# A two-layer encoder trunk: the second layer's input product by one Strassen level on fp16 parts, its weights prepared and the up product's weight sums made by GpSimd

## The chip, the cores and the metric

The kernel runs on one core of one Trainium2 chip. The metric is the device time of one execution in microseconds; of three runs of the kernel before, the median is 2181.28 us (2181.2 to 2181.32). Engines are called by their names or short names: TensorE (PE, with its weight loads as PEld), VectorE (DVE), ScalarE (ACT), GpSimd (POOL) and SyncE (SP).

## The reference

1024 tokens of width 1024 pass two layers. Each layer has an attention with low-rank queries and keys beside a convolution module, then a gated feed-forward block with a short convolution. Cut to what is computed:

```python
D_MODEL, SEQ, DEPTH, D_FF = 1024, 1024, 2, 2816
for l in range(DEPTH):
    h = _rmsnorm(x, g_mix[l])
    p = h @ w_in[l]                       # 384 + 256 + 32 + 512 + 512 columns
    q = _rmsnorm(p[..., :o1], g_q[l]) @ w_uq[l]          # 8 heads, 64 + 32 rope
    kv = _rmsnorm(p[..., o1:o2], g_kv[l]) @ w_ukv[l]     # 8 heads, 64 + 64
    k_rope = _apply_rope(p[..., o2:o3], cos, sin)
    y_attn = _mla_attention(q_nope, q_rope, k_nope, k_rope, v)
    a, gt = jnp.split(p[..., o3:], 2, axis=-1)
    u = _dwconv(a * jax.nn.sigmoid(gt), w_dw_conv[l], b_dw_conv[l])   # 31 taps
    u = jax.nn.silu(_layernorm(u, g_conv_ln[l], b_conv_ln[l]))
    x = x + jnp.concatenate([y_attn, u], axis=-1) @ w_o[l]
    h2 = _rmsnorm(x, g_ffn[l])
    z = _dwconv(h2 @ w_up[l], w_dw_ffn[l], b_dw_ffn[l])  # 3 taps
    zg, zv = jnp.split(z, 2, axis=-1)
    x = x + (jax.nn.silu(zg) * zv) @ w_down[l]
return _rmsnorm(x, g_final)
```

The change concerns `h @ w_in[1]`, the second layer's input product, and the weights of the first layer's `h2 @ w_up[0]`.

## The kernel before, in words

**Form.** Everything is held transposed: channels on the 128 partitions, 1024 tokens in the free direction, in two halves of 512. The order of instructions on each engine is the order in which the program issues them. In the feed-forward block that order comes from an agenda: `put(step, rank, f)` files an action under one of TensorE's products (a step, about 2.6 us), and after each product its actions are issued by rank.

**Precision.** Each float32 operand is split into an upper and a lower part (hi, lo), and each product is three passes: hi by hi, hi by lo, lo by hi.

**Stages of a layer.** *Project*: the input product in 14 sections (gates g0 to g3, values a0 to a3 of the convolution, kv0 and kv1, the rope key kr, q0 to q2), then the keys k, queries' rope part u, queries n and values v, while the 31-tap convolution runs beside it. *Attention* of 8 heads, then the *output product* wo. *Up product*: 22 pairs of column groups, f = 0 to 21, each a gate half (e = 0) and a value half (e = 1) of 128 columns. *Down product*, whose results are added to x.

**The up product** is one Strassen level on fp16 parts: seven products of half size for each f, in the order (1, 2, 6, 5, 7, 3, 4) from f = 4 on, each 12 matmuls of 128x512 (L1306), 84 for an f. Products 1 and 2 use the weight block as it comes, the other five use sums of blocks. `raw[f][e]` (tiles `wu`) holds the fetched float32 block, and its sums are made in place, one after another, by DMAs that GpSimd issues and that add to the tile (`add_in`, L1196: `sum5`, `sum6`, `sum3`, `sum7`). After each, ScalarE scales and rounds the upper part (L1267), and VectorE makes the lower part (L1270), into tiles `w`. ScalarE takes the squares of each block (L1212); their total over partitions gives a power-of-two scale (`own_total`, `own_scale`). The results are evicted by ScalarE and VectorE (L1313, L1314), the three filter taps are VectorE's (L1766, tiles `o` and `v`), and L1186 holds `sub`, an addition of two tiles. The next block's sums begin while the former's products run.

**The second layer's input product** (`next_sections`, `inputs`, `shared_key`) is not Strassen. A section is 48 matmuls in float32 round form (L245, L558, L564), kr 32 (L810). The weights come by a casting DMA on GpSimd's queue (`cast`, L204); ScalarE writes the negative (L208) and a second, accumulating DMA makes the lower part (L209, `complete`). The moving operand is x times the gain g, split by L1732 and L1733 (`norm_apply`). The root of the mean square is found beside that (`norm_root`, L284 to L303), spread over the partitions (L322) and multiplied into the results as the row scale rx when they leave PSUM (L649, L652, L679, and in `key_rope`).

**The 31-tap convolution.** Near taps (NEAR_TAPS 12, 14, 15, 14 for the four channel groups, 55 in all) are VectorE's (`conv_step`, L2039). Far taps: ScalarE scales (L2045) and a DMA issued by GpSimd adds (L2046). Late taps, in the attention: GpSimd scales (L2056) and adds, either by itself (L2059) or by a DMA (L2061). Order and amounts come from tables and from a clock that the program counts up as it issues.

**The down product** (L1551) is Strassen too. Its last results are added to x by VectorE, x is stored, and the norm for the next layer is begun: squares, transposes and the root for the left half before the product ends, the right half after it.

Of the kernel before, what the change touches and what calls it, by code (L numbers as in the profile page):

```python
# [18 lines left out]
T = 1024  # L19
D = 1024  # L20
DEPTH = 2
# [102 lines left out]
WARM = 8  # L124

# [19 lines left out]
class Encoder:  # L145
# [32 lines left out]
    def weight_source(self, l, name):  # L178
        a = self.a
        kind, j = name[:-1], name[-1]  # L180
        if name == "kr":
            return a["w_kr"][l]
# [220 lines left out]
    def run(self):  # L403
# [11 lines left out]
        self.xd = [a["x"], self.dp.tile([8, 128, T], F32, name="x_mid")]  # L415
        carry = None
# [117 lines left out]
    def next_sections(self, l, nxt, supply):  # L534
        names = ("g0", "a0", "g1")
        w = [self.complete(*e) for e in nxt["w"]]
        for k in range(8):
            self.norm_apply(l, nxt["x"], nxt, 1, k)
        self.norm_sums(l, nxt["x"], nxt, 1, range(4, 8))
        supply(-16.0)  # L540
        self.pp.tile([128, T], F32, name=f"skip{l}", tag="w1", bufs=1)
        ps = [self.wide(f"p{n}{l}") for n in names]
        for c in range(2):
            for i in range(3):
                if (c, i) == (0, 0):
                    self.upper_first(ps[i], self.tiled(w[i]), nxt["hl"], HALVES[c])
                for k in range(8 if c or i else 0):
                    self.partial(ps[i], self.tiled(w[i]), nxt["hl"], k, (c,))
                if c == 1 and i == 0:
                    self.norm_root(l, nxt, 1, self.bank)  # L550
                if c == 1 and i == 1:
                    self.norm_spread(l, nxt, 1, self.bank)
        return nxt["hl"], nxt["r"], dict(zip(names, ps))

# [12 lines left out]
    def project(self, l, carry):  # L567
# [12 lines left out]
        outs = [(OUT_FROM + OUT_STEP * i, i, None) for i in range(4)]  # L580
        col = lambda i, n=1: qk[:, i:i + n]
# [19 lines left out]
        def key_scale():  # L601
            sums = self.bank(f"kt{l}", (128, 3))
# [40 lines left out]
        def start(steps):  # L643
            next(steps)
            active.append([clock["pe"] + 1.8, steps, 99])

# [8 lines left out]
        def glu(j):  # L655
# [7 lines left out]
            taps.extend((j, t) for t in todo[:NEAR_TAPS[j]])  # L663
            taps.sort(key=lambda e: NEAR_ORDER.index(e[0]))
            away[j] = todo[NEAR_TAPS[j]:]
# [11 lines left out]
        def latent(name, out, key, j):  # L677
            c = self.blk(f"c{name}{l}")
# [13 lines left out]
        def keys_norm():  # L692
            r = st["rkv"] = self.blk(f"rkv{l}")
            for s, p in zip(HALVES, self.spread(rooted("kroot"), f"rkv{l}", HALVES, self.bank)):
                nc.scalar.copy(out=r[:, s], in_=p)
# [1508 lines left out]
```

## Time and profile before

| | |
|---|---|
| median of three runs | 2181.28 us |
| span of the profiled execution | 2179.0 us |
| clock granted to TensorE in it | 1.00 in all but the last stage (0.99) |
| project, first layer | 0 to 200 us |
| attention, output product | 200 to 402, to 485 us |
| up product, first layer | 485 to 885 us |
| down product, first layer | 885 to 1087 us |
| project, second layer: input product | 1087 to 1239 us |
| keys, queries and values | 1239 to 1281 us |
| attention, output product | 1281 to 1470, to 1566 us |
| up product, second layer | 1566 to 1966 us |
| down product, last norm | 1966 to 2179 us |
| GpSimd's L1196 in the first up product | 80 DMA issues, 70.0 us |

The profiled execution's own time is its span; it lies 2.3 us below the median of the runs. Times in the text are from the span's start. A row of a group gives the line, engine and operation, the output and input tiles with numbers left out, their shapes and the count, then busy time and mean duration; a row of the timeline gives start and duration of single instructions, with the idle time before and what ended it in brackets.

### The profile page before, as it was taken

How to read it: one execution, taken by the hardware profiler on the slowest of the kernel's cores; microseconds unless marked ns; L12 is line 12 of the kernel's file. 1: busy time of each engine (PE TensorE's matmuls, PEld its weight loads, DVE VectorE, ACT ScalarE, POOL GpSimd, SP SyncE). 2: the span in 40 equal slices, each digit the busy share in tenths (PEclk: the TensorE clock that was granted, in tenths of full speed). 3: DMA queues.
4: the chain of work that ended last, by engine and by line, in shares of the span. 5: the costliest groups of instructions: out<-in, count | busy, mean ns of one | idle time of the engine just before them, and what ended most of it. 6: DMA issues, size and time to landing. Idle time of an engine off the chain costs nothing.

```text
span 2179.0 us, 29766 instructions
## 1 busy us (share of the span) xinstructions
PE 2169.7 (100%) x10722; PEld 1260.7 (58%) x10722; DVE 1844.7 (85%) x2531; ACT 1456.6 (67%) x2183; POOL 537.2 (25%) x534
## 2 busy tenths in 40 slices
PE   9999999999999999999999999999999999999998
PEld 8887665754444444644488876667544444446445
DVE  6989999879998887887859789998898888878877
ACT  6455888746898886554623668886478888865544
POOL 1223777211111111000012355771112111110000
PEclk9999999999999999999999999999999999999999
DMA  6898878754688885554578986886646888856533
GB/s 195 184 187 212 164 152 171 245 163 104 149 244 259 222 261 145 193 178 151 166 177 164 188 207 134 159 186 200 175 100 164 261 241 242 241 141 218 182 111 122
DMA packets 163013, 400.96 MB, mean 184 GB/s; under 512 B 21888, under 2 KB 29936, under 8 KB 162864
## 3 DMA queue, kind: packets, MB, share of 16 engines
q0 software_dynamic: 62528, 145.89, 36.4%
q1 hardware_dynamic: 100048, 252.63, 33.8%
q8 instruction: 84, 1.38, 0.3%
q10 hardware_dynamic: 288, 0.53, 0.1%
q14 instruction: 65, 0.53, 0.1%
HBM read 270.75 MB, written 69.66 MB: 156 GB/s over the span
## 4 chain that ended last, share of the span: by engine, by line
PE 98%; ACT 1%; DVE 1%; issue 0%; DMA 0%; DVEq 0%; ACTq 0%
PE p L1306 36%; PE pd L1551 18%; PE po L1026 7%; PE s L1818 7%; PE t L1858 5%; PE pq L245 3%; PE pa L245 3%; PE o L1880 2%; PE pkv L245 2%; PE pg L245 2%; PE pg L564 2%; PE pn L245 2%; PE o L1885 1%; PE pv L1794 1%; PE pk L245 1%; PE pa L564 1%
## 5 line engine op out<-in xcount | busy, mean ns | idle before, releaser
L1306 PE MATMUL p<-b,w 128*128 128x512 f16 x3696 | 800.0, 379 | 0.2
L1306 PEld LDWEIGHTS <-w 128*128 128x128 f16 x3696 | 358.7, 98 | 431.9 <-issue 0.8
L1551 PE MATMUL pd<-ab,wd 128*128 128x512 f16 (+2 forms) x1920 | 404.2, 373 | 0.0
L1196 POOL DMA_DIRECT2D wu<-in_w_up x176 | 152.2, 879 | 770.2 <-DVE w L1270 581.5
L1551 PEld LDWEIGHTS <-wd 128*128 128x128 f16 x1656 | 161.9, 98 | 179.4 <-issue 0.5
L1818 PE MATMUL s<-k,q 96*128 96x512 f16 x768 | 186.9, 379 | 0.0
L1270 DVE SCALAR_TENSOR_TENSOR w<-wu,wf,w 128x512 f16<-128x512 f32 (+1 forms) x216 | 177.2, 834 | 3.6 <-ACT w L1267 3.6
L1861 DVE SCALAR_TENSOR_TENSOR pt<-t,pt 128x512 f16<-128x512 f32 x256 | 163.0, 676 | 10.0 <-ACT pt L1860 9.0
L1267 ACT ACTIVATE w<-wu,wf 128x512 f16<-128x512 f32 (+1 forms) x216 | 164.8, 781 | 0.1
L1860 ACT ACTIVATE pt<-t 128x512 f16<-128x512 f32 x256 | 139.1, 596 | 32.0 <-PE t L1858 30.0
L1820 DVE TENSOR_REDUCE mx<-s 128x1 f32<-128x1024 f32 x128 | 155.0, 1211 | 1.0 <-PE s L1818 1.0
L1540 ACT ACTIVATE ab<-ac,ds 128x512 f16<-128x512 f32 x108 | 75.5, 717 | 108.7 <-DVE ac L1455 73.0
L1828 ACT ACTIVATE p<-s,mx 128x1024 f32<-128x1024 f32 x128 | 143.3, 1120 | 2.2 <-DVE mx L1820 1.8
L2039 DVE SCALAR_TENSOR_TENSOR conv<-gate,par,conv 128x1009 f32<-128x1009 f32 (+14 forms) x110 | 139.9, 1274 | 3.1 <-ACT conv L659 0.4
L2056 POOL TENSOR_SCALAR late<-gate,par 128x1019 f32<-128x1019 f32 (+13 forms) x99 | 135.5, 1368 | 27.2 <-PE pn L245 13.9
L1858 PE MATMUL t<-ident,p 128*128 128x128 f32 x1024 | 136.6, 275 | 0.9 <-ACT p L1828 0.6
L1858 PEld LDWEIGHTS t<-ident,p 128*128 128x128 f32 x1024 | 116.8, 141 | 34.8 <-issue 7.4
L1766 DVE SCALAR_TENSOR_TENSOR o<-zg,par,o 128x1023 f32<-128x1023 f32 x88 | 112.7, 1281 | 8.9 <-ACT o L1760 7.4
L1314 DVE SCALAR_TENSOR_TENSOR zg<-p,wf,zg 128x512 f32<-128x512 f32 x72 | 54.0, 750 | 71.2 <-PE p L1306 61.6
L1766 DVE SCALAR_TENSOR_TENSOR v<-zv,par,v 128x1023 f32<-128x1023 f32 x88 | 112.1, 1276 | 0.0
L1818 PEld LDWEIGHTS <-q 96*128 96x128 f16 x768 | 74.0, 97 | 64.6 <-issue 2.1
L1541 DVE SCALAR_TENSOR_TENSOR ab<-ac,ds,ab 128x512 f16<-128x512 f32 x108 | 79.9, 748 | 19.2 <-ACT ab L1540 19.2
(2179 smaller groups left out, 3814.1 us busy)
## 6 DMA issues: line engine op xcount, KB each, us to landing
wu<-in_w_up SPq DMA_DIRECT2D x98, 512.0 KB
wu<-in_w_up POOLq DMA_DIRECT2D x176, 256.0 KB, 4.8
sd<-in_w_down SPq DMA_DIRECT2D x44, 512.0 KB
ws<-sd SPq DMA_DIRECT2D x44, 512.0 KB
act<-v SPq DMA_DIRECT2D x36, 512.0 KB
ac<-act SPq DMA_DIRECT2D x72, 256.0 KB
wo<-in_w_o POOLq DMA_DIRECT2D x32, 256.0 KB, 7.7
x_mix<-y SPq DMA_DIRECT2D x32, 256.0 KB
```

Of the source, the lines that this page charges most:

```text
L245: nc.tensor.matmul(ps[:, HALVES[c]], w, x[:, HALVES[c]], start=(k == 0 and s == 0), stop=(k == n - 1 and s == 2))
L1026: self.nc.tensor.matmul(ps, p[:, sl], q[:, cs], start=(k == 0 and t == 0), stop=(k == 3 and t == 2))
L1196: nc.gpsimd.dma_start(out=dst, in_=src, accum_op=ALU.add)
L1267: nc.scalar.activation(out=t, in_=src, func=AF.Copy, scale=scale[f])
L1270: nc.vector.scalar_tensor_tensor(out=t, in0=src, scalar=scale[f], in1=hi, op0=ALU.mult, op1=ALU.subtract)
L1306: nc.tensor.matmul(ps, w[p][:, k * 128:(k + 1) * 128], b[:, q], start=(i in (1, 5, 2) and k == 0 and t == 0), stop=(k == 3 and t == 2), sk ...
L1551: nc.tensor.matmul(ps[t, m][:, cs], w[i, j][p][:, m * 128:(m + 1) * 128], b[:, q, cs], start=(i in (1, 5, 2) and j == 0 and s == 0), stop= ...
L1766: self.nc.vector.scalar_tensor_tensor(out=o[:, a:b], in0=z[:, at + a:at + b], scalar=self.par[l][:, tap:tap + 1], in1=o[:, a:b], op0=ALU.m ...
L1818: nc.tensor.matmul(ps[:, cs], q[0:96, i, qs], k[0:96, j, cs], start=(s == 0), stop=(s == 2))
L1820: nc.vector.tensor_reduce(out=mx, in_=ps, op=ALU.max, axis=AX.X, negate=True)
L1858: nc.tensor.transpose(tp[:, i, qi * 128:(qi + 1) * 128], st["p"][2 * qp + qi][:, kt * 128:(kt + 1) * 128], self.ident)
L1861: nc.vector.scalar_tensor_tensor(out=lo, in0=tp, scalar=P_SCALE, in1=hi, op0=ALU.mult, op1=ALU.subtract)
```

## The change

**The product.** For the second layer the 14 sections become seven column pairs (`PAIRED`): (g0, a0) to (g3, a3), (kv0, kv1), (q0, kr), (q1, q2); kr is padded to 128 columns. Each pair is one Strassen level of seven products, 49 in all in the order `PAIR_ORDER`, of 12 fp16 matmuls each. They run in `opening`, before the pool of PSUM tiles of the first layer's feed-forward is given back. `next_sections` goes.

**The moving operand.** x is multiplied by gain, a scale, and the root (`set_norm`) before it is split, so the results need no row scale. Its Strassen sums are made on VectorE (`set_mix`), the upper parts by ScalarE, the lower parts by VectorE (`set_end`).

**The weights.** They are prepared during the first layer's up product, a pair at each f of `PREPARE_AT`: SyncE fetches two blocks of 512 KB, ScalarE takes two squares, the scale comes with the up product's own (`own_total` has four columns there), GpSimd scales, combines, casts and subtracts (14 instructions for a pair), and SyncE stores the fp16 parts in DRAM (`win`, four stores), whence they are read back when needed.

**The up product's sums.** In the first layer, for f from 4 on, `sum5`, `sum6` and `sum3` are additions by GpSimd (`on_pool`) in place of accumulating DMAs; `sum7` stays a DMA.

**The convolution in the second layer.** 37 near taps (`PAIR_NEAR`) in place of 55; `side` gives GpSimd late taps during the projection, with its own sum, and far taps between; 52 late taps are left for the attention in place of 49. A step that a later product needs is brought forward by `settle`.

```diff
+PAIRED = (("g0", "a0"), ("g1", "a1"), ("g2", "a2"), ("g3", "a3"), ("kv0", "kv1"), ("q0", "kr"), ("q1", "q2"))
+PREPARED = ((1, 2), (5, 4), (6, 3), (7,))
+PREPARE_AT = (4, 7, 10, 13, 16, 18, 20)
+PAIR_NEAR = (11, 8, 10, 8)
...
+            def product(i, f):
...
+                for k in range(4):
+                    b = sets[i][k]
+                    for s, (x, y) in enumerate(((0, 0), (0, 1), (1, 0))):
+                        nc.tensor.matmul(p, t[:, x, k * 128:(k + 1) * 128], b[:, y], start=(i in (1, 5, 2) and k == 0 and s == 0),
+                                         stop=(k == 3 and s == 2), skip_group_check=i in (6, 7, 4, 3))
...
+            put(1, 3, lambda: self.norm_root(l, nxt, 1, lambda name: self.pp.tile([128, 512], F32, name=name, tag="d4", bufs=1)), 2.5)
+            put(2, 3, lambda: self.norm_spread(l, nxt, 1, lambda name: self.pp.tile([128, 512], F32, name=name, tag="d5", bufs=1)))
+            for i, ns in PAIR_MIX.items():
+                for e, n in enumerate(ns):
+                    put(n, 3, lambda i=i, e=e: mix(i, e), 1.2 * (i in (5, 3)) + 1.15 * (i != 3))
+                    put(n + 1, 2.5, lambda i=i, e=e: self.set_end(nxt, i, e), 1.28)
...
+                    if pool[0] <= clock["pe"]:
+                        next(self.tap_late(l, j, away[j].pop(0), u[j], conv[j], "both"), None)
+                        pool[0] = far_at[j] = clock["pe"] + 4.2
+                    elif more:
+                        self.tap_far(l, j, away[j].pop(0), u[j], conv[j])
...
+        def on_pool(f, h):
+            t = raw[f][1][:, left]
+            nc.gpsimd.tensor_tensor(out=t, in0=t, in1=raw[f][h[0]][:, HALVES[h[1]]], op=ALU.add)
+
         def sum5(f):
+            if ahead and f >= LEFT:
+                return on_pool(f, (1, 1))
             add_in(raw[f][1][:, left], block(f, 1, 1))
...
+            def scaled(e):
+                nc.gpsimd.tensor_scalar(out=two[e], in0=two[e], scalar1=z(33 + q), scalar2=1.0, op0=ALU.mult, op1=ALU.mult)
...
+            def hi(i):
+                src, k = both(i)
+                made[i] = self.blk(f"wit{q}{i}", F16, (128, k, 2, 512))
+                nc.gpsimd.tensor_copy(out=made[i][:, :, 0], in_=src)
+
+            def lo(i):
+                src, k = both(i)
+                nc.gpsimd.tensor_tensor(out=made[i][:, :, 1], in0=src, in1=made[i][:, :, 0], op=ALU.subtract)
+
+            def store(i):
+                nc.sync.dma_start(out=self.win[q][i], in_=made.pop(i))
...
+            work = ([lambda: scaled(0)], [lambda: scaled(1)], [lambda: hi(0)], [lambda: lo(0)],
+                    [lambda: plus(part(0, 0), part(1, 0)), lambda: hi(3)], [lambda: lo(3), lambda: plus(part(1, 0), part(1, 1))],
+                    [lambda: hi(1)], [lambda: lo(1), lambda: plus(part(0, 0), part(1, 1))],
+                    [lambda: plus(part(0, 1), part(0, 0)), lambda: hi(2)], [lambda: lo(2)])
...
+    def set_norm(self, nxt, c, k):
+        xk = nxt["x"][k][:, HALVES[c]]
+        self.nc.vector.scalar_tensor_tensor(out=xk, in0=xk, scalar=self.wz[:, k:k + 1], in1=nxt["r"][:, HALVES[c]],
+                                            op0=ALU.mult, op1=ALU.mult)
...
+    def set_end(self, nxt, i, e):
+        two, src = nxt["half"].pop((i, e))
+        self.nc.vector.tensor_tensor(out=two[:, :, 1], in0=src, in1=two[:, :, 0], op=ALU.subtract)
```

**How the order moves.** In the first layer's up product, about f = 12 to 15, GpSimd's queue before holds only DMA issues. `wu0_131` is the value half of f = 13 in the first layer; the last number is that of the allocation.

```order
L1196 DMA wu0_120_6219<-in_w_up 128x512
L1196 DMA wu0_131_6380<-in_w_up 128x512
L1196 DMA wu0_141_6539<-in_w_up 128x512
L1196 DMA wu0_131_6380<-in_w_up 128x512
L1196 DMA wu0_130_6378<-in_w_up 128x512
L1196 DMA wu0_141_6539<-in_w_up 128x512
L1196 DMA wu0_151_6694<-in_w_up 128x512
```

At the same place GpSimd's queue now reads so; `wi30` and `wi31` are the two blocks of the fourth column pair of the next layer, `wit30` and `wit33` their fp16 parts, `wz` the scales:

```order
L1378 TENSOR_TENSOR wu0_121_6341<-wu0_121_6341,wu0_120_6339 128x512
L1462 TENSOR_SCALAR wi30_6464<-wi30_6464,wz_103 128x1024
L1462 TENSOR_SCALAR wi31_6466<-wi31_6466,wz_103 128x1024
L1374 DMA wu0_120_6339<-in_w_up 128x512
L1378 TENSOR_TENSOR wu0_131_6516<-wu0_131_6516,wu0_130_6514 128x512
L1472 CAST wit30_6748<-wi30_6464 128x2x512
L1476 TENSOR_TENSOR wit30_6748<-wi30_6464,wit30_6748 128x2x512
L1378 TENSOR_TENSOR wu0_141_6683<-wu0_141_6683 128x512
L1449 TENSOR_TENSOR wi30_6464<-wi30_6464,wi31_6466 128x512
L1472 CAST wit33_6801<-wi30_6464 128x512
L1476 TENSOR_TENSOR wit33_6801<-wi30_6464,wit33_6801 128x512
L1449 TENSOR_TENSOR wi31_6466<-wi31_6466 128x512
```

Three of each block's four sums (L1378) have become instructions of GpSimd's own, and the preparation of the next layer's weights stands between them, ahead of sums that come later; the fourth sum is still a DMA (L1374).

In the second layer's projection, behind the input product, GpSimd's queue before holds weight fetches (`wk1`, `wu21`, `wq21`) and the adding DMAs of the far taps (`conv1_0` to `conv1_2` are the running sums of channel groups 0 to 2, and the number behind `far1_0` is the tap):

```order
L204 DMA wk1h_10535<-in_w_k 128x4x256
L209 DMA wq21l_10482<-in_w_in 128x1024
L2046 DMA conv1_0_10048<-far1_0_17_10590 128x1022
L2046 DMA conv1_1_10112<-far1_1_17_10593 128x1022
L2046 DMA conv1_2_10262<-far1_2_17_10596 128x1022
L204 DMA wu21h_10624<-in_w_uq 128x2x384
L209 DMA wk1l_10536<-in_w_k 128x4x256
```

There it now reads so, with the late taps' scalings (L2379, formerly L2056) and sums (L2382, formerly L2059) in between:

```order
L2379 TENSOR_SCALAR late1_0_14_10784<-zg0_10077,par1_183 128x1023
L2382 TENSOR_TENSOR conv1_0_10404<-conv1_0_10404,late1_0_14_10784 128x1023
L2379 TENSOR_SCALAR late1_2_11_10827<-zg2_10171,par1_183 128x1020
L2382 TENSOR_TENSOR conv1_2_10510<-conv1_2_10510,late1_2_11_10827 128x1020
L2369 DMA conv1_0_10404<-far1_0_16_10830 128x1023
L223 DMA wu21h_10860<-in_w_uq 128x2x384
L228 DMA wk1l_10757<-in_w_k 128x4x256
L2379 TENSOR_SCALAR late1_2_12_10881<-zg2_10171,par1_183 128x1021
L2382 TENSOR_TENSOR conv1_2_10510<-conv1_2_10510,late1_2_12_10881 128x1021
L2369 DMA conv1_0_10404<-far1_0_17_10918 128x1022
```

The weight fetches of the keys and queries (L223, L228, formerly L204, L209) now stand behind instructions of GpSimd's own.

398 lines of the change are left out of this document (322 added, 76 removed).

## The prediction

> **What bounds the kernel now.** I read the page's busy times first, then the chain that ended last, then the windows, then groups inside one stage.
>
> ```profile
> PE 2169.7 (100%) x10722; PEld 1260.7 (58%) x10722; DVE 1844.7 (85%) x2531; ACT 1456.6 (67%) x2183; POOL 537.2 (25%) x534
> PE 98%; ACT 1%; DVE 1%; issue 0%; DMA 0%; DVEq 0%; ACTq 0%
> L1306 PE MATMUL p<-b,w 128*128 128x512 f16 x3696 | 800.0, 379 | 0.2
> ```
>
> TensorE is busy for 2169.7 of 2179.0 us and carries 98% of the chain. The up products (L1306) wait 0.2 us in all. So every matmul taken out is worth its full time, and every new wait of TensorE costs its full time. Next, who keeps TensorE supplied, by stage (columns: length, then busy PE, PEld, DVE, ACT, POOL with counts, clock, DMA share, GB/s):
>
> ```profile
> 540.00:867.00 327.00, 326.88 (x1531) 148.31 (x1529) 280.93 (x395) 267.54 (x392) 62.04 (x71) 1.00 0.78 215
> 1087.00:1281.00 194.00, 193.71 (x877) 160.30 (x876) 151.20 (x162) 81.45 (x103) 45.99 (x52) 1.00 0.80 177
> 1281.00:1470.00 189.00, 188.57 (x1156) 114.82 (x1156) 171.90 (x226) 156.86 (x285) 135.98 (x112) 1.00 0.79 170
> ```
>
> The first row is the first layer's up product from the fifth column pair on: 18 pairs (f = 4 to 21). The second is the second layer's projections, the third its attention. In the up product VectorE has only 327.0 - 280.9 = 46.1 us free, and what it makes (lower weight parts, filter taps, evictions) is what TensorE waits for next.
>
> **The change part by part.** *TensorE.* One input section is 48 matmuls of 128x512, the rope section 32, one column pair of the up product 84:
>
> ```profile
> 1131.76 10.88 PE pg L245 x48
> 1197.04 7.25 PE pkr L810 x32
> 620.70 18.15 PE p L1306 x84
> ```
>
> Thirteen sections and the rope section go: 13 x 10.88 + 7.25 = 148.7 us for 656 matmuls at 0.227. In come 7 x 7 products of 12 matmuls, 588, of the up product's form at 18.15 / 84 = 0.216: 127.0 us. Gain 21.6 us. The transposes for the norm's root stay, four and four. With all else hidden the span would be 2179.0 - 21.6 = 2157.4. The profile's span lies 2.3 us under the median of the timed runs (2181.28), which I take as what lies around it: 2159.7.
>
> *The operand sets at the opening.* VectorE must scale the right half and make five combined sets in time:
>
> ```profile
> 1109.50 0.69 DVE L295 TENSOR_REDUCE rx_512v<-rx_512t 128x4 f32<-128x512 f32 x1 [13.18 <-PE rx_512t L284]
> 1111.42 0.16 DVE L300 SCALAR_TENSOR_TENSOR rx_512y<-rx_512q,rx_512y 128x4 f32<-128x4 f32 x1
> 1087.95 0.74 DVE L1733 SCALAR_TENSOR_TENSOR xs_0l<-x,par,xs_0h 128x512 fp32r<-128x512 f32 x1
> 1088.07 0.73 ACT L1732 ACTIVATE xs_7h<-x,par 128x512 fp32r<-128x512 f32 x1 [0.97 <-DVE x L1456]
> ```
>
> The root took 2.1 us (1109.50 to 1111.58). After the change its transposes follow two products (5.2 us), the scale is spread at about 9.3 us, and then come 8 norms (0.66 us start to start), 8 combinations and 10 lower parts of 1024 columns (1.14, group L1186 v below) and 8 evictions (0.66): 8 x 0.66 + 18 x 1.14 + 8 x 0.66 = 31 us, done near 40 us. The last set is needed at 16 products, 42 us. It fits, if narrowly; at the end of the first layer four lower parts (4.6 us) press against 3 us of free time. I take 1 us for both, between 0 and 4 (no gain is possible where TensorE does not wait now).
>
> *GpSimd in the up product.* This is the large term. It now makes 54 sums (three for each of 18 column pairs) in place of 54 DMA issues, and 98 instructions of weight preparation (14 for each of seven pairs). Its prices, from the attention and the last stage:
>
> ```profile
> 1321.35 2.34 POOL L2059 TENSOR_TENSOR conv<-conv,late 128x1016 f32<-128x1016 f32 x1
> 1323.67 1.10 POOL L2056 TENSOR_SCALAR late<-gate,par 128x1016 f32<-128x1016 f32 x1
> 2168.57 2.96 POOL L1738 TENSOR_TENSOR x<-x,rx 128x256 f32<-128x256 f32 x4 [222.70 <-ACT rx L1720]
> ```
>
> Two inputs cost 2.34 us for 1016 columns and 0.74 for 256; in between, 1.27 for 512. The sums are 54 x 1.27 = 69 us. A pair needs two scalings (1.10), casts of 3.5 x 1024 columns (no cast is in the trace; bounds 1.10 for one input and 2.34 for two; I take 1.10, as it has one input), subtractions of 3.5 x 1024 (3 x 2.34 + 1.27) and four sums (1.27): 2.2 + 3.9 + 8.3 + 5.1 = 19.5 us, for seven 136 us. Together 205 us of GpSimd in the 327 us where it issued DMAs alone. [...]
>
> GpSimd alone has room for 205 us. VectorE beside it has not. The one place in this trace where GpSimd computes next to VectorE instructions with both inputs in SBUF:
>
> ```profile
> 1269.83 1.22 DVE L798 SCALAR_TENSOR_TENSOR qns<-qn,qns 128x1024 f16<-128x1024 f32 x1
> 1274.65 3.06 DVE L798 SCALAR_TENSOR_TENSOR qns<-qn,qns 128x1024 f16<-128x1024 f32 x2
> 1277.63 1.21 DVE L794 TENSOR_TENSOR qn<-pn,rq 128x1024 f32<-128x1024 f32 x1
> 1280.01 2.23 DVE L798 SCALAR_TENSOR_TENSOR qns<-qn,qns 128x1024 f16<-128x1024 f32 x1 [1.17 <-ACT qns L796]
> ```
>
> ```profile
> 1274.36 1.14 POOL L2056 TENSOR_SCALAR late<-gate,par 128x1023 f32<-128x1023 f32 x1 [13.91 <-PE pn L245]
> 1276.41 2.25 POOL L2056 TENSOR_SCALAR late<-gate,par 128x1020 f32<-128x1020 f32 x1
> 1278.75 2.39 POOL L2059 TENSOR_TENSOR conv<-conv,late 128x1020 f32<-128x1020 f32 x1
> 1281.13 2.10 POOL L2056 TENSOR_SCALAR late<-gate,par 128x1019 f32<-128x1019 f32 x1
> ```
>
> L798 alone takes 1.22. At 1280.01 it met a running GpSimd sum and took 2.23: it ended 1.10 after that sum's end at 1281.14. GpSimd's next scaling took 2.10 instead of 1.10: it ended 0.99 after L798's end at 1282.24. They took turns. L794, one input of which is in PSUM, kept its 1.21 beside GpSimd. From 1274.36 to 1283.23, 8.87 us, stand three scalings, one sum and three L798, alone 3 x 1.10 + 2.34 + 3 x 1.22 = 9.30: the pair needs 0.95 of the two times added. In the up product VectorE does mostly the work that takes turns (12 column pairs, 620.70 to 838.56):
>
> ```profile
> L1270 DVE SCALAR_TENSOR_TENSOR w<-wu,wf,w 128x512 f16<-128x512 f32 x61 | 44.5, 746 | 0.6 <-ACT w L1267 0.6
> L1766 DVE SCALAR_TENSOR_TENSOR v<-zv,par,v 128x1023 f32<-128x1023 f32 x25 | 31.9, 1275 | 0.0
> L1766 DVE SCALAR_TENSOR_TENSOR o<-zg,par,o 128x1023 f32<-128x1023 f32 x24 | 30.8, 1282 | 1.3 <-ACT o L1760 0.7
> L1270 DVE SCALAR_TENSOR_TENSOR w<-wu,wf,w 128x1024 f16<-128x1024 f32 x12 | 15.3, 1276 | 0.0
> L1186 DVE TENSOR_TENSOR v<-v,o 128x1024 f32<-128x1024 f32 x12 | 14.6, 1217 | 0.0
> L1186 DVE TENSOR_TENSOR sd<-sd,sd 128x512 f32<-128x512 f32 x21 | 14.4, 685 | 0.0
> L1186 DVE TENSOR_TENSOR sd<-sd 128x512 f32<-128x512 f32 x21 | 14.4, 685 | 0.0
> 620.70:838.56 217.86, 217.86 (x1021) 98.86 (x1020) 186.59 (x272) 181.15 (x269) 41.95 (x48) 1.00 0.85 243
> ```
>
> These have two SBUF inputs: 165.9 us as recorded, 0.76 us in each us of the stage; since neighbours overlap by some 8% (0.66 from start to start at a record of 0.75), 153 us. Times 1.5 for 18 pairs: 230 us that take turns, and 281 - 230 = 51 us (evictions from PSUM, small ones) that need not. Taking turns, 0.95 x (230 + 205) = 413 us against 327: 86 us over, even if GpSimd fills every other moment of VectorE. If it fills none, 281 + 205 - 327 = 159 us. GpSimd's order is fixed and each sum stands behind preparation, so none of the 205 us can move to a later stage. I take 100 us, near the lower end, as the runs of PSUM work are short but frequent. The new waits also block: a sum waits on GpSimd for VectorE's lower part, and behind it stand preparation, the one sum left as a DMA and the stores that SP issues; ScalarE's next upper part, and so TensorE, waits for the sum.
>
> [...]
>
> *The second layer's projections.* 16 taps now go over GpSimd there, 15 of them with its own sum: 16 x 1.10 + 15 x 2.34 = 53 us, within the last 124 us of the stage. VectorE loses 18 taps of 55 and all products with the row scale, and gains three evictions a pair; by the same prices its order holds about 108 us in those 124, some 77 with two SBUF inputs. Taking turns, 0.95 x (77 + 53) = 124: just enough; with nothing beside, 108 + 53 - 124 = 37 over. I take 10. The k, u and v weights are issued behind these taps on GpSimd.
>
> *Hidden edits.* ScalarE's 14 squares (1.05 and 0.19, some 16 us) lie under the 327 - 267.5 = 59 us it is free. The seven small scale chains on VectorE are 5 us of 46. DMA gains 20 MB and loses 14 at a share of 0.78: hidden. In the attention GpSimd gets three taps more of 49, at 136 of 189 us busy, beside VectorE work that reads PSUM: hidden.
>
> Sum: 2159.7 + 100 + 10 + 1 = 2271, given as 2270.
>
> **The rivals.** (a) *Hidden after all, faster.* The collisions shown are few and short. If VectorE wins nearly every turn and GpSimd's work slips into the 51 + 46 us and beyond without making its sums late, the 21.6 us stay: 2160 to 2168. It decides below 22 us of net delay, that is, if less than a third of GpSimd's 205 us (22 + 46) falls on VectorE's two-input work. Against it: 230 us of 327 are such work, and every collision in these rows cost one side the other's remainder. Chance 0.16. (b) *Half the price.* GpSimd's 512-wide and cast instructions run nearer to one-input cost, 110 us in all. Then the turns need 0.95 x (230 + 110) = 323 us, and only bad moments cost, 25 to 75 us: 2185 to 2240. For it: half of its instructions are forms that the trace lacks. Against: 0.74 us at 256 columns. Chance 0.21. (c) *Nothing measurable:* the delay just meets 21.6 us. Chance 0.03; 0.2% (4 us) is about what a measurement of this kernel can tell from no change. That the change fails to remove matmuls is no rival: 588 stand in its order.
>
> **How the numbers follow.** The forecast, VectorE and GpSimd taking turns, has 0.60, at 2240 to 2340 (86 us alone gives 2246; 159 and half of the projections' 37 give 2338). Slower: 0.60 + 0.21 = 0.81; faster 0.16. The range reaches from the lower edge of (b) and (c), 2180, to 2340 and leaves out (a) and a little on top.
>
> **What would show it.** Right: in the up product lower parts (L1270's successor) and taps well over 0.75 and 1.28 us, GpSimd scalings over 1.10, VectorE busy near 100%, and TensorE's up products waiting some 100 us for VectorE's weights; the input product itself at about 127 us. Wrong: these instructions at their old durations beside a GpSimd busy for 200 us, or TensorE waiting for GpSimd's sums, weights of the second layer, or the sets at the opening instead.

## The result and the profile after

The changed kernel takes 2315.47 us (median of four runs, 2314.92 to 2316.39) against 2181.24 (four runs of the kernel before): 1.0615 times as long, 95% interval 1.060 to 1.063. Its profiled execution has a span of 2313.3 us, 134.3 more than before. By the first and last matmuls of each stage in the trace, 98.0 us of it lie in the first layer's up product (400.7 to 498.7), 34.6 in the second layer's projection with its values (207.7 to 242.3) and 1.4 in the down product.

From the page of the changed kernel: busy times, TensorE's granted clock in 40 slices, the shares of the chain, and the up products.

```profile
PE 2193.6 (95%) x10654; PEld 1205.2 (52%) x10654; DVE 1999.4 (86%) x2576; ACT 1475.8 (64%) x2223; POOL 833.5 (36%) x641
PEclk9999999999998899999999989999999999999999
PE 72%; DVE 13%; issue 5%; ACT 5%; POOL 4%; DMA 1%; SPq 0%; DVEq 0%; ACTq 0%; POOLq 0%
L1549 PE MATMUL p<-b,w 128*128 128x512 f16 x3696 | 830.0, 387 | 66.7 <-ACT zg L1556 33.8
```

TensorE carries 72% of the chain, not 98%, and VectorE and GpSimd are on it. TensorE's busy time rose although its work shrank: in two stages the clock is below full. The windows say where (length, busy PE, PEld, DVE, ACT, POOL with counts, clock, DMA share, GB/s): the up product from the fifth column pair on, then three parts of the projection.

```profile
540.00:966.00 426.00, 359.45 (x1543) 154.25 (x1542) 403.71 (x422) 280.29 (x419) 297.11 (x168) 0.93 0.54 177
1187.00:1244.00 57.00, 47.23 (x212) 20.95 (x211) 41.44 (x53) 23.24 (x35) 0.00 (x0) 0.97 0.37 115
1244.00:1357.30 113.30, 91.83 (x405) 41.17 (x404) 85.36 (x70) 47.28 (x60) 64.58 (x39) 0.89 0.52 125
1357.30:1408.50 51.20, 41.06 (x175) 32.56 (x173) 50.65 (x46) 24.36 (x28) 37.17 (x23) 0.92 0.80 189
```

In the first row VectorE is busy for 95% of the stage. The groups of that stretch show why; L1513 is the lower part (formerly L1270), L2089 the filter tap (L1766), L1378 the sum on GpSimd, L1476 and L1462 the preparation's subtraction and scaling.

```profile
L1513 DVE SCALAR_TENSOR_TENSOR w<-wu,wf,w 128x512 f16<-128x512 f32 x87 | 98.3, 1143 | 3.4 <-ACT w L1510 3.4
L2089 DVE SCALAR_TENSOR_TENSOR o<-zg,par,o 128x1023 f32<-128x1023 f32 x41 | 91.9, 2241 | 4.4 <-ACT o L2083 4.2
L1378 POOL TENSOR_TENSOR wu<-wu,wu 128x512 f32<-128x512 f32 x36 | 70.8, 1967 | 96.8 <-DVE w L1513 96.8
L1476 POOL TENSOR_TENSOR wit<-wi,wit 128x1024 f16<-128x1024 f32 x21 | 58.0, 2764 | 0.6
L1462 POOL TENSOR_SCALAR wi<-wi,wz 128x1024 f32<-128x1024 f32 x13 | 26.9, 2074 | 0.0
```

A lower part takes 1.14 us instead of about 0.75, a tap in this group 2.24 instead of 1.28. A few rows of the timeline in that stage show how (start, duration):

```profile
842.03 1.63 DVE L1513 SCALAR_TENSOR_TENSOR w<-wu,wf,w 128x1024 f16<-128x1024 f32 x1
...
842.54 3.11 POOL L1476 TENSOR_TENSOR wit<-wi,wit 128x1024 f16<-128x1024 f32 x1
...
844.25 1.96 DVE L1513 SCALAR_TENSOR_TENSOR w<-wu,wf,w 128x512 f16<-128x512 f32 x1
845.61 1.72 POOL L1449 TENSOR_TENSOR wi<-wi,wi 128x512 f32<-128x512 f32 x1
846.12 1.75 DVE L1364 TENSOR_TENSOR sd<-sd 128x512 f32<-128x512 f32 x1
```

Here the engines take turns: each instruction ends a little less than its solo duration after the end of the other engine's. The subtraction ends at 845.65, the lower part that started under it at 846.21, GpSimd's sum at 847.33, VectorE's addition at 847.87: 0.56, 1.12 and 0.54 us, where alone they take 0.75, 1.26 and 0.69. At other places VectorE gets no turn between GpSimd's instructions:

```profile
851.46 6.06 DVE L2089 SCALAR_TENSOR_TENSOR o<-zg,par,o 128x1023 f32<-128x1023 f32 x1
851.55 1.57 POOL L1378 TENSOR_TENSOR wu<-wu,wu 128x512 f32<-128x512 f32 x1
852.78 2.43 POOL L1476 TENSOR_TENSOR wit<-wi,wit 128x1024 f16<-128x1024 f32 x1
854.87 1.56 POOL L1378 TENSOR_TENSOR wu<-wu 128x512 f32<-128x512 f32 x1
```

This tap stands through three instructions of GpSimd and ends 1.09 us after the third. Three taps of the stretch take 6.04 to 6.06 us like that.

I split TensorE's loss by the steps between the starts of neighbouring matmuls: what goes over 0.6 us is a wait (less 0.216), and steps of 0.3 to 0.6 us between matmuls of 128x512 are slow clock. In the up product that gives 73.1 us in 32 waits and 25.1 us over 124 slow matmuls, 98.2 together; in the projection 43.6 and 14.2 us, which less the 21.6 us of saved matmuls is 36.2, against 34.6 measured. The kernel before has no such wait in these two stages and under 2 us of such steps. What TensorE waits for in the up product (total, times, longest):

```profile
PE p L1549 <- ACT zg L1556: 33.8, 16, 6.1
PE p L1549 <- DVE w L1513: 24.0, 11, 4.7
PE p L1549 <- DVE zv L1557: 8.5, 4, 3.9
```

### The profile page after: what moved, and what is told of

Its sections match the earlier page's. It is cut to its first block, busy times and chain, and to the rows that moved or that the text cites. A ratio compares the mean times of both kernels' runs of the same rounds, so it can differ in the third digit from the quotient of the medians.

```text
span 2313.3 us, 29968 instructions
## 1 busy us (share of the span) xinstructions
PE 2193.6 (95%) x10654; PEld 1205.2 (52%) x10654; DVE 1999.4 (86%) x2576; ACT 1475.8 (64%) x2223; POOL 833.5 (36%) x641
## 4 chain that ended last, share of the span: by engine, by line
PE 72%; DVE 13%; issue 5%; ACT 5%; POOL 4%; DMA 1%; SPq 0%; DVEq 0%; ACTq 0%; POOLq 0%
PE p L1549 20%; PE pd L1819 17%; PE po L1202 7%; PE s L2141 7%; PE t L2181 5%; PE pi L930 3%; DVE w L1513 2%; PE o L2203 2%; DVE v L2089 1%; PE pq L264 1%; PE pa L264 1%; PE o L2208 1%; POOL wit L1476 1%; PE pv L2117 1%; POOL wi L1449 1%
## 5 line engine op out<-in xcount | busy, mean ns | idle before, releaser
L1549 PE MATMUL p<-b,w 128*128 128x512 f16 x3696 | 830.0, 387 | 66.7 <-ACT zg L1556 33.8
L1549 PEld LDWEIGHTS <-w 128*128 128x128 f16 x3696 | 363.4, 99 | 525.1 <-issue 69.5
L1374 POOL DMA_DIRECT2D wu<-in_w_up x122 | 105.2, 883 | 495.9 <-DVE w L1513 390.7
L1513 DVE SCALAR_TENSOR_TENSOR w<-wu,wf,w 128x512 f16<-128x512 f32 (+1 forms) x216 | 218.5, 1024 | 5.2 <-ACT w L1510 5.2
L2379 POOL TENSOR_SCALAR late<-zg,par 128x1021 f32<-128x1021 f32 (+14 forms) x68 | 100.9, 1484 | 289.5 <-PE pi L930 286.6
L2089 DVE SCALAR_TENSOR_TENSOR o<-zg,par,o 128x1023 f32<-128x1023 f32 x88 | 152.1, 1728 | 8.9 <-ACT o L2083 7.8
L2089 DVE SCALAR_TENSOR_TENSOR v<-zv,par,v 128x1023 f32<-128x1023 f32 x88 | 125.9, 1433 | 5.4 <-ACT v L2083 5.4
L1378 POOL TENSOR_TENSOR wu<-wu,wu 128x512 f32<-128x512 f32 x36 | 70.8, 1967 | 96.8 <-DVE w L1513 96.8
L2382 POOL TENSOR_TENSOR conv<-conv,late 128x1020 f32<-128x1020 f32 (+13 forms) x37 | 97.7, 2640 | 10.1 <-DMA conv<-late 4.3
L1809 DVE SCALAR_TENSOR_TENSOR ab<-ac,ds,ab 128x512 f16<-128x512 f32 x108 | 79.8, 748 | 19.5 <-ACT ab L1808 19.5
```

What stands on the lines that cost most here:

```text
L1513: nc.vector.scalar_tensor_tensor(out=t, in0=src, scalar=scale[f], in1=hi, op0=ALU.mult, op1=ALU.subtract)
L1549: nc.tensor.matmul(ps, w[p][:, k * 128:(k + 1) * 128], b[:, q], start=(i in (1, 5, 2) and k == 0 and t == 0), stop=(k == 3 and t == 2), sk ...
L2089: self.nc.vector.scalar_tensor_tensor(out=o[:, a:b], in0=z[:, at + a:at + b], scalar=self.par[l][:, tap:tap + 1], in1=o[:, a:b], op0=ALU.m ...
```

## The experiments

Theory 1 is the prediction's: GpSimd and VectorE take turns in SBUF. Theory 2, the rival: GpSimd is slow by itself and works in order, so sums, or their DMA issues, come late behind the preparation.

**Prices, each by itself.** A kernel of its own that computes nothing of the reference. The sentences of it that matter:

```python
dve_sum:  nc.vector.tensor_tensor(out=vb, in0=va, in1=vb, op=ALU.add)              # 1024, L35
dve_psum: nc.vector.scalar_tensor_tensor(out=vb[:, 0:512], in0=pv, scalar=sc, in1=va[:, 0:512], ...)  # L38
g_sum:    nc.gpsimd.tensor_tensor(out=gb[:, 0:512], in0=gb[:, 0:512], in1=ga[:, 0:512], op=ALU.add)   # L41
g_fill:   nc.gpsimd.memset(gd, 1.0)                                                # 1024, L53
```

> A kernel of its own that leaves out the whole computation: each form of the up product alone, then VectorE's sum of two SBUF tiles (1024 columns) and VectorE's eviction from PSUM beside each form of GpSimd, then 48 matmuls of 128x512 after ever longer pauses of TensorE. Theory 1 (GpSimd and VectorE take turns in SBUF): alone, GpSimd's sum of 512 columns takes about 1.3 us, the scaling and the cast of 1024 about 1.1 to 1.2, the subtraction of 1024 about 2.4, VectorE's sum 1.22; side by side, GpSimd reading SBUF and VectorE's sum take the two durations added for one of each (2.2 us for VectorE's sum beside the short ones, up to 3.5 beside the subtraction); beside a fill, which reads nothing, and beside the eviction from PSUM, every instruction keeps its own duration. Theory 2 (GpSimd is itself as slow as the changed kernel shows it, 1.97 us a sum and 2.76 a subtraction, and its place in line is what costs): GpSimd's durations alone are already those, and VectorE's do not change beside it. Pauses: after a pause of 2 us or more the next matmuls run at 0.43 us start to start for a few us and then at 0.216; without a pause at 0.216 throughout.

The timeline of this kernel, runs of one instruction joined (start, duration of all, count). First VectorE's sum alone, GpSimd's sum alone; then the two side by side; VectorE's sum beside fills; VectorE's eviction from PSUM beside GpSimd's sums.

```profile
17.55 7.52 DVE L35 TENSOR_TENSOR vb<-va,vb 128x1024 f32<-128x1024 f32 x6
30.20 7.96 POOL L41 TENSOR_TENSOR gb<-gb,ga 128x512 f32<-128x512 f32 x6
71.00 29.87 POOL L41 TENSOR_TENSOR gb<-gb,ga 128x512 f32<-128x512 f32 x14
71.15 33.32 DVE L35 TENSOR_TENSOR vb<-va,vb 128x1024 f32<-128x1024 f32 x16
201.94 14.06 POOL L53 MEMSET gd<- 128x1024 f32 x14
202.11 20.11 DVE L35 TENSOR_TENSOR vb<-va,vb 128x1024 f32<-128x1024 f32 x16
222.49 18.70 POOL L41 TENSOR_TENSOR gb<-gb,ga 128x512 f32<-128x512 f32 x14
222.64 12.53 DVE L38 SCALAR_TENSOR_TENSOR vb<-pv,s,va 128x512 f32<-128x512 f32 x16
```

Alone, single instructions take 1.22 us (VectorE's sum), 1.26 (GpSimd's sum), 1.12 (scaling), 1.04 (cast), 2.12 (subtraction of 1024), 0.95 (fill). Side by side VectorE's sum takes 2.17 and GpSimd's 2.12, strictly in alternation, one of each in 2.20 us, 0.89 of the two durations added; with the scaling, the cast and the subtraction in its place one of each takes 2.06, 1.97 and 3.06 us, 0.87 to 0.92. Beside fills and beside evictions from PSUM each keeps its own: from start to start VectorE's sum takes 1.26 us beside fills (1.25 alone), the eviction 0.78 beside GpSimd's sums (0.78 alone), GpSimd's sum 1.34 beside evictions (1.33 alone). Theory 1 holds instruction by instruction, and theory 2's premise falls: GpSimd's sum is 1.26 us by itself; the 1.97 of the changed kernel lie between that and the 2.12 beside VectorE.

The same kernel lets TensorE pause. After a pause of 4.03 us (weight loads of 128x512 matmuls, one for each):

```profile
335.92 0.10 PEld L81 LDWEIGHTS <-w 128*128 128x128 f16 x1 [4.31 <-issue]
336.30 0.15 PEld L81 LDWEIGHTS <-w 128*128 128x128 f16 x1 [0.28 <-issue]
...
341.37 1.18 PEld L81 LDWEIGHTS <-w 128*128 128x128 f16 x6 [0.23 <-issue]
```

Thirteen matmuls run 0.43 us apart, then 0.216; the 0.28 us of "issue" ahead of each load go with the slow clock. The 5% of "issue" on the changed kernel's chain are something else: of these 113 us only 4.7 fall on slow matmuls, and most of the others on time in which VectorE, ScalarE or GpSimd is still running the instruction before. After pauses of 1.84, 2.57, 3.30, 4.03 and 5.47 us there were 0, 8, 13, 13 and 9 slow matmuls.

**Parts taken out of the up product.** Three runs of the changed kernel: its sums as DMAs again; the preparation left out (a constant is stored in place of the weights); and the preparation replaced by fills, which take GpSimd's time but read nothing (the weights are constants here too).

```diff
 def sum5(f):                                  # sums as DMAs; sum6 and sum3 alike
-    if ahead and f >= LEFT:
+    if False:
         return on_pool(f, (1, 1))
```

> The changed kernel with the up product's 54 sums by accumulating DMAs again; the preparation stays on GpSimd. Theory 1 (turns): 230 us of VectorE and 136 of GpSimd by solo prices need 0.95 x 366 = 348 us in a stage of 327, so the up product loses 21 to 60 of its 98 us instead of all: 2235 to 2280 us. Theory 2 (the sums are late in GpSimd's line): the issues still stand behind the preparation, so nearly all of the loss stays: 2290 to 2320 us.

```diff
-    nc.sync.dma_start(out=self.win[q][i], in_=made.pop(i))      # preparation left out
+    nc.sync.dma_start(out=self.win[q][i], in_=self.fill[:, 0:len(PREPARED[i])])
-    for k, fs in enumerate(work): ...
```

> The changed kernel with the GpSimd instructions that prepare the second layer's weights left out (a constant is stored in their place; fetches, squares, stores and scales stay), the 54 sums stay on GpSimd. Theory 1 (turns): 230 + 69 us take 0.95 x 299 = 284 of 327 us, so the up product loses 0 to 25 us: 2215 to 2245 us in all, the projection's loss of about 30 us staying. Theory 2 (line): the sums stand behind nothing then, and take 2 us each where a DMA takes 5: no loss in the up product, 2215 us; VectorE's lower parts (L1513) stay near 1.13 us by neither, by theory 1 they take about 0.9, by theory 2 their 0.75.

```diff
-    nc.gpsimd.tensor_scalar(out=two[e], in0=two[e], scalar1=z(33 + q), ...)     # fills
+    nc.gpsimd.memset(two[e], 0.01)
...                                                                         # casts and block sums alike
-    nc.gpsimd.tensor_tensor(out=made[i][:, :, 1], in0=src, in1=made[i][:, :, 0], op=ALU.subtract)
+    nc.gpsimd.memset(made[i], 0.02)
```

> The changed kernel with each of the 14 GpSimd instructions of a weight pair replaced by fills of the same tiles, which read nothing (the weights get constants): by the prices measured alone (0.95 us for a fill of 1024 columns of float32, taken as about 1.9 for 2048 of fp16) about 19 us a pair where the preparation alone is 2 x 1.12 + 3.5 x 1.04 + 3 x 2.12 + 1.26 + 4 x 1.26 = 18.5. GpSimd is held as long, at the same places in its order. Theory 1 (turns in SBUF): the fills hold VectorE up nowhere, and the up product loses what it loses without a preparation, 7 us, or up to 20 where the sums wait in line: 2225 to 2240 us. Theory 2 (place in GpSimd's line): the sums come as late as before and most of the 98 us stays: 2290 to 2320 us.

Measured: 2297.19 us with the sums as DMAs (ratio to before 1.0532, 1.050 to 1.056), 2225.60 without the preparation (1.0203, 1.017 to 1.023), 2242.67 with fills (1.0282, 1.025 to 1.031). The whole up product in the windows, sums as DMAs:

```profile
485.30:962.10 476.80, 422.29 (x1876) 184.94 (x1875) 447.07 (x508) 323.97 (x485) 234.22 (x178) 0.95 0.73 209
```

Without the preparation:

```profile
485.00:892.60 407.60, 402.23 (x1876) 182.29 (x1875) 371.45 (x509) 323.59 (x485) 120.73 (x80) 1.00 0.64 209
```

With fills:

```profile
484.80:907.30 422.50, 405.54 (x1876) 182.97 (x1875) 375.60 (x508) 324.41 (x485) 241.24 (x206) 0.99 0.62 202
```

Of 98 us above 400.7, the preparation alone makes 76.1, the sums alone 6.9, and the fills with the sums 21.8. Without the preparation a lower part of 512 columns takes 0.80 us, between the 0.9 of theory 1 and the 0.75 of theory 2. The fills hold GpSimd for 133 us, as long as the preparation would by itself (130), and VectorE's busy time is 375.6 with them, 371.5 without: it hardly notices them. So of the preparation's part, 76 us (498.7 to 422.5) come from reading SBUF, and 15 (407.6 to 422.5) from standing in GpSimd's line: theory 1 for the most part, theory 2 for a small one. The first run lies where theory 2 expected it and misses theory 1's range: I had expected 21 to 60 of the 98 us to stay, and 76 did. But the fills tell the two apart, and what was wrong is my size: the preparation alone costs nearly its ceiling (281 + 130 - 327 = 84), not its floor.

**Spread out.** The preparation over 20 products instead of 10, sums as DMAs.

```diff
-    put(n + 2 + k, 9, g)
+    put(n + 2 + 2 * k, 9, g)
...                                           # the stores likewise
```

> The changed kernel with the 54 sums as DMAs (2297 us) and, beside that, each pair's preparation spread over 20 products in place of 10. A theory of crowding: in the 10 products (26 us) of a preparation GpSimd asks 18.5 us and VectorE's two-input work 0.7 x 26 = 18, 10.5 us more than there are, and 7 x 10.5 = 74 us, which is what was lost; over 20 products (52 us) it is 18.5 + 36.4, 3 us too much, 21 in all: about 2245 us. If single long instructions in GpSimd's line, not the crowd, delay the sums' issues, their number is the same and the loss stays above 60 us: above 2285 us.

2290.13 us (1.0499, 1.047 to 1.053), the up product 471.6 with VectorE at 450.6. The theory of crowding falls: 7 us went, 52 were expected. VectorE's busy time tells more. It is 344.0 us before, 347.4 with all of GpSimd's computing out (the change's small scale chains), 371.5 with the sums, 447.1 with the preparation, 450.6 with it spread, 464.6 with both. The preparation stretches VectorE by 100 us of its own 130, wherever it lies. That agrees with the kernel before, where 0.76 of each microsecond is VectorE work with two SBUF inputs (0.76 x 130 is 99). The 54 sums, 68 us by themselves, stretch it by 24 only. In the changed kernel GpSimd's idle time ahead of the 54 ends 24 times with a VectorE lower part (L1513, 96.8 us), so such a sum may meet few of VectorE's instructions at a time; that is argued, not shown.

**The projection.** GpSimd's taps left out there (the scalings and the sums are not computed):

```diff
-    next(self.tap_late(l, j, away[j].pop(0), u[j], conv[j], "both"), None)
+    away[j].pop(0)
```

> The changed kernel with GpSimd's taps in the second layer's projection left out (scalings and sums; far taps by ScalarE and DMA stay). From the end of the down product to the values the changed kernel takes 221 us, the kernel before 190. If turns of these taps with VectorE make most of that, it falls to about 195 us and the whole to about 2288 us; if the opening sets and the order on ScalarE make it, it falls by less than 8 us and the whole stays above 2305 us.

2285.58 us (1.0478, 1.045 to 1.051). The groups of the projection behind the opening, changed kernel: VectorE's near taps and GpSimd's sums.

```profile
L2362 DVE SCALAR_TENSOR_TENSOR conv<-zg,par,conv 128x1009 f32<-128x1009 f32 (+10 forms) x34 | 61.6, 1817 | 0.6
L2382 POOL TENSOR_TENSOR conv<-conv,late 128x1020 f32<-128x1020 f32 (+6 forms) x17 | 50.9, 2992 | 2.9 <-DMA conv<-far 1.5
```

And the near taps without GpSimd's:

```profile
L2362 DVE SCALAR_TENSOR_TENSOR conv<-zg,par,conv 128x1009 f32<-128x1009 f32 (+10 forms) x33 | 41.7, 1270 | 0.6
```

The taps are back at 1.27 us, some 20 us less of VectorE's time, and the span is 28.5 shorter: this half of the projection's loss goes with GpSimd's taps. That it is turns rests on the durations, as no run puts fills in the taps' place. Weights that come late behind the taps in GpSimd's line are not it: no wait of TensorE in the changed kernel's projection names a weight fetch. The other half stays, 21.4 us of waits and 5.3 of slow clock.

**All of GpSimd's computing out**, preparation and taps left out, sums as DMAs:

> The changed kernel with sums as DMAs, without GpSimd's preparation (a constant is stored) and without GpSimd's taps in the second layer's projection (left out): all of GpSimd's own computing that the change added, gone. Theory 1: the up product is back at 401 us, the projection keeps what the sets at its opening and the order on ScalarE cost (26 us in the run without taps, 21 of them waits), which just eats the gain of 21.6 us in TensorE's work: 2183 to 2192 us. If the 26 us came from DMAs or weights that were late because of the up product, it goes below 2175.

2194.49 us (1.0057, 1.003 to 1.008), 2.5 above what I gave: the up product still loses 3.6. The product's gain of 21.6 is eaten in the projection. TensorE's waits there in this run:

```profile
PE pi L930 <- ACT zg L938: 7.0, 1, 7.0
PE pi L930 <- ACT zv L938: 4.0, 2, 3.3
PE rx_512t L303 <- DVE xss L284: 2.5, 1, 2.5
PE pi L930 <- DVE zg L939: 2.2, 2, 1.6
```

**The opening.** In the changed kernel VectorE makes a set like this (L2060 combines, L2044 is the lower part):

```profile
1222.12 1.23 DVE L2044 TENSOR_TENSOR in<-x,in 128x1024 f16<-128x1024 f32 x1 [1.11 <-ACT in L2038]
1223.27 1.22 DVE L2060 SCALAR_TENSOR_TENSOR x<-x,x 128x1024 f32<-128x1024 f32 x1
1225.60 1.23 DVE L2044 TENSOR_TENSOR in<-x,in 128x1024 f16<-128x1024 f32 x1 [1.11 <-ACT in L2038]
```

Between a combination and its lower part VectorE stands idle for 1.11 us while ScalarE makes the upper part. Issued behind the next combination instead, beside everything left out as in the run before:

```diff
-    put(n + 1, 2.5, lambda i=i, e=e: self.set_end(nxt, i, e), 1.28)
+    put(n + 1, 3.5, lambda i=i, e=e: self.set_end(nxt, i, e), 1.28)
```

> The run without GpSimd's preparation and taps (2194 us) and, beside that, the lower part of each Strassen set of x issued on VectorE behind the next set's combination instead of ahead of it. That run's waits of TensorE at the 10th to 15th product add up to 6.9 us (3.45 + 0.89 + 1.74 + 0.79). If VectorE's wait for ScalarE's upper part in the chain of sets makes them, they go, with a slow-clock stretch of some 2 us behind them: 2184 to 2188 us. If VectorE has simply too much to do there, they stay: 2193 to 2195 us.

The same place then:

```profile
1123.72 1.22 DVE L2023 TENSOR_TENSOR in<-x,in 128x1024 f16<-128x1024 f32 x1
1124.86 1.22 DVE L2039 SCALAR_TENSOR_TENSOR x<-x,x 128x1024 f32<-128x1024 f32 x1
1125.99 1.22 DVE L2023 TENSOR_TENSOR in<-x,in 128x1024 f16<-128x1024 f32 x1
```

2185.75 us (1.0022, 1.001 to 1.003): 8.7 gone, all waits from the 10th to the 15th product among them. The latency through ScalarE was the cause.

**The eviction behind the rope key.** The 7.0 us of the run with everything left out, on its timeline: PE's product at 1230.78 waits for an eviction that stands on ScalarE behind the rope key's copy (L742), square (L745) and two upper parts.

```profile
1223.48 1.04 ACT L742 COPY krt<-zv 32x1024 f32<-32x1024 f32 x1 [0.60 <-DVE zv L739]
1226.94 1.05 ACT L745 ACTIVATE krt<-zv 32x1024 f32<-32x1024 f32 x1 [2.41 <-DVE zv L744]
...
1230.07 0.66 ACT L938 ACTIVATE zg<-pi,wz 128x512 f32<-128x512 f32 x1
...
1230.78 4.60 PE L930 MATMUL pi<-in,win62t 128*128 128x512 f16 x12 [7.03 <-ACT zg L938]
```

In the changed kernel the same wait is 12.8 us. The key's copy and square issued later:

```diff
+            if l:
+                yield 2.5, 0.3
             nc.scalar.copy(out=t2[0:32, :], in_=t[32:64, :])
-            yield 5.0, 1.5
+            yield 0.0 if l else 5.0, 1.5
...                                          # the square alike
```

> The run with interleaved sets and, beside that, the rope key's copy and square on ScalarE issued some 2.5 us later, when VectorE has made what they read. The wait of 7.2 us at the 44th product (an eviction on ScalarE that stands behind them in line) and its slow clock should go: 7 to 9 us less than the run with interleaved sets, 2175 to 2180 us, which is less than the kernel before by some 3 us. If that eviction was late for another reason (VectorE's own half of it), no more than 2 us go.

2182.72 us (1.0008, 0.9998 to 1.0017), 3.0 less, not 7 to 9: the wait shrank to 4.0 us, but the projection has 7.7 us of slow clock, 4.9 in the run before. The place is right, the cure is half of one. Even with none of the price on GpSimd paid, and the sets mended, the change only meets the kernel before; and in these runs nothing prepares the weights.

**Full versions without GpSimd's computing.** Sums as DMAs; upper parts of the prepared weights by ScalarE, lower parts by VectorE, block sums by accumulating DMAs; taps by ScalarE and DMA; interleaved sets.

```diff
-    nc.gpsimd.tensor_copy(out=made[i][:, :, 0], in_=src)
+    nc.scalar.activation(out=made[i][:, :, 0], in_=src, func=AF.Copy, scale=z(33 + q))
-    nc.gpsimd.tensor_tensor(out=made[i][:, :, 1], in0=src, in1=made[i][:, :, 0], op=ALU.subtract)
+    nc.vector.scalar_tensor_tensor(out=made[i][:, :, 1], in0=src, scalar=z(33 + q), in1=made[i][:, :, 0], op0=ALU.mult, op1=ALU.subtract)
...
-    plus = lambda o, x: nc.gpsimd.tensor_tensor(out=o, in0=o, in1=x, op=ALU.add)
+    plus = lambda o, x: nc.gpsimd.dma_start(out=o, in_=x, accum_op=ALU.add)
```

> A version to keep the Strassen product without GpSimd's computing: sums as DMAs; each pair's upper parts by ScalarE and lower parts by VectorE straight from the float32 blocks with the scale in the instruction, the four block sums by accumulating DMAs, spread over 20 products; GpSimd's taps of the projection by ScalarE and DMA; at the opening each lower part of a set behind the next set's combination, so that VectorE does not wait for ScalarE. Theory 1: VectorE gets 7 x 4 lower parts, 3.5 x 1.28 x 7 = 31 us, in the 46 us it has free, the up product loses 0 to 15 us, and the opening about 8 us of its 12: 2165 to 2190 us in all. If VectorE's free time is no more to be had (bursts), the up product loses 30 us and more: above 2200 us.

2254.29 us (1.0335, 1.031 to 1.037): missed, the up product takes 452.1. The waits there name ScalarE:

```profile
PE p L1545 <- ACT zg L1552: 31.2, 14, 5.0
```

```profile
ACT wit L1470 <- DMA wi<-wi: 14.1, 5, 5.0
ACT wit L1470 <- DMA wi<-in_w_in: 12.1, 5, 3.2
```

VectorE has 377.3 us of work in 401, as counted, but ScalarE stands before an upper part until its DMA sum has landed, and the evictions that TensorE needs stand behind it. With longer spacing, the later rope key and half the taps:

```diff
-    for i, h, g in ((0, 2, 3), (1, 7, 8), (3, 10, 11), (2, 18, 19)):
+    for i, h, g in ((0, 2, 3), (1, 8, 9), (3, 11, 12), (2, 23, 24)):
...                                          # the block sums' places likewise
-    pool[0] = far_at[j] = clock["pe"] + 4.2
+    pool[0] = far_at[j] = clock["pe"] + 8.4
```

> A full version again: sums as DMAs, upper parts by ScalarE, lower parts by VectorE, block sums by accumulating DMAs with 5 to 6 products between a sum and its use (3 to 5 in the version before, where ScalarE waited 27 us for them), interleaved sets, the later rope key, and every second tap of GpSimd in the projection by ScalarE and DMA, the others left to the attention. By VectorE's count the up product holds: 344 + 31 + 3 of 401 us; if ScalarE's waits were the cause of the 51 us there, 5 to 20 us stay; the projection gains 21.6 and gives 5 to 15 back to taps: 2170 to 2200 us. If the up product's order has no room for 28 more parts whatever their spacing, above 2225 us.

2210.40 us (1.0129, 1.011 to 1.014), 105 less than the changed kernel and 10 above the range I gave. The up product takes 425.9; TensorE's wait for ScalarE's evictions there is 13.8 us in place of 31.2. No version here beats the kernel before.

## Why the prediction was right, and where it was not

**TensorE's gain, 21.6 us: right.** A product of 12 matmuls starts 2.59 us after the one before wherever nothing holds it up, which is 0.216 a matmul.

**GpSimd in the up product: 100 taken, 98.0 measured, by two errors that met, which is luck.** The mechanism is shown: the price run has the turns, and the run with fills takes 76 of the 98 us away with the reading. The prices were close: a pair's preparation is 18.5 us (19.5 in the prediction), a sum 1.26 (1.27), the cast 1.04 (1.10), together 198 against 205. But the waits are 73.1 us, under the floor of 86: with 198 us at 0.95 it would be 0.95 x 428 - 327 = 80, and TensorE's waits make it 400 of 428, 0.93. Nor was 0.95 the price of two busy engines: the 8.87 us that it was read from hold 1.17 us of idle VectorE and the 1.21 us of L794, which does not compete. The price run has 0.89, by which the floor would be 0.89 x 428 - 327 = 54, less than was measured. The other 25.1 us are slow clock behind the waits, a term that the sum did not have at all. Nor does the sum of both parts follow from each: the floor gives 15 for the preparation alone (0.95 x 360 - 327), and 76.1 were measured (59.0 in waits). The step that fails is that GpSimd's work would fall first into VectorE's other moments: the preparation stretched VectorE by 100 us of its 130, so it met two-input work in about the share that such work has of the time (0.76). Nor do turns always go one for one, as some of VectorE's instructions stand through two or three of GpSimd's in a row (6.06 us for a tap of 1.28). What decides who goes next, and how the parts combine (76 and 7, but 98 together), stays open.

Reading SBUF is what counted: beside GpSimd's sums VectorE's sum took 2.17 us in the price run, beside fills, which only write, 1.22, as alone. The run with fills agrees, with VectorE busy for 375.6 us in the up product against 371.5 without them. The slow clock came after 2.57 us of idleness in the price run, and in the changed kernel's up product a lone wait of 2.20 brought 8 slow matmuls where one of 2.33 brought none, so no single length of a wait decides it.

**The opening sets, 1 us (0 to 4): wrong.** "31 us, done near 40 us" added VectorE's durations and left out that each set goes to ScalarE and back. The last set was done 54 us after the down product. Up to the 15th product TensorE waited 10.7 us, of which interleaving takes the last 5.2; 5.6 us up to the first transposes stay.

**The projection's taps, 10 us (0 to 37): the right mechanism, the size too low.** 28.5 us went with them. "Just enough" by added work was no measure: a chain of small steps on VectorE and ScalarE (root, norms, rope key, upper parts) stands in line behind the stretched taps, late ones stop TensorE, and the longer stops bring the slow clock. The wait at the 44th product, 12.8 us, was in no term.

**In all** the forecast of 2270 was 45 us low, all of it in the projection: about 56 us lost there beside the gain, 11 forecast. The signs named beforehand came true for taps, lower parts, scalings and VectorE's busy share (95%); TensorE waited as much for ScalarE's evictions (33.8 us) as for VectorE's weights (24.0) and evictions (8.5), and the input product took 170.5 us, not 127. The rival "hidden" falls with VectorE's 117 us of added busy time in the up product, "half the price" with the prices alone.

## What to carry to other kernels

An engine with 75% of its time free, as GpSimd had, was no free engine when its instructions read SBUF next to VectorE work with two SBUF inputs: count nearly every microsecond of it that meets such work as one of VectorE's, wherever it is spread (130 us of preparation kept VectorE busy 100 us longer, and 103 when spread over twice the products). Beside fills and beside VectorE's evictions from PSUM these runs show no such price (1.22 us for VectorE's sum beside fills, 0.75 for its eviction beside GpSimd's sums, as alone). And a stage in which TensorE never waited lost twice when it began to: in the changed kernel slow matmuls added a third to the waits (25.1 us to 73.1, 14.2 to 43.6). A chain that crosses engines must be sized by its latency, not by one engine's sum.

## What the runs showed of the hardware

Where both read SBUF and VectorE has two inputs there, GpSimd and VectorE hold each other up. In the price run they alternate, one instruction each, at 0.87 to 0.92 of the added durations (2.20 us for 1.22 and 1.26). In the changed kernel they do not always: three taps stood through three GpSimd instructions in a row (6.04 to 6.06 us in place of 1.28). TensorE's half-speed clock can follow a pause of little more than 2 us (after 1.84 us none, after 2.57 us 8 matmuls at 0.43 us; in the changed kernel a lone wait of 2.20 us brought it and one of 2.33 did not). After a single pause of the price run it lasted for 8 to 13 matmuls of 128x512.
